# Casting the high weight parts a group ahead of the low parts in a hybrid retention and RWKV-7 decoder step

## The chip, the core and the metric

One NeuronCore of a Trainium2 chip runs the whole program in one launch. The metric is the device time in microseconds. Three runs of the kernel before gave 2919.16, 2921.64 and 2923.35 us; the median is 2921.64 us. Five engines work in parallel, each in the order of its own queue: TensorE (PE, with its weight loads as PEld), VectorE (DVE), ScalarE (ACT), GpSimd (POOL) and SyncE (SP), which issues every DMA here. An instruction whose semaphores are not there yet holds up everything behind it on its engine.

## The reference

Two layers of a decoder run on 256 new positions of one sequence and on 8 decode tokens, 264 columns in all, in float32. Cut to what matters:

```
xn = rms_norm(h, g_attn)
proj = xn @ w_mix                         # retention q, k, v, gate; RWKV r, k, v and low-rank inputs
y_ret = retention_mixer(...)              # 8 heads of 128, chunks of 128
y_rw = rwkv7_mixer(...)                   # 16 heads of 64, S = S*w + sa (kk*a)^T + v k^T
h = h + concat(y_ret, y_rw) @ w_out
hn = rms_norm(h, g_ffn)
h = h + (silu(hn @ w_gate) * (hn @ w_up)) @ w_down
```

The outputs are the normalised h and the new states of both mixers and of the token shift.

## The kernel before

**The weight stream.** All weights lie in DRAM as 128x128 blocks in the order of use, 6624 of them. `Stream` loads eight at a time (512 KB, tile `w_raw`) and splits them four at a time; four blocks are called a group here. ACT casts a group to the high part `w_hi` in float32r (L96), then DVE takes `w_raw` minus `w_hi` as the low part `w_lo` (L99; POOL for the first four groups). TensorE multiplies each block in three passes: high part by the high part of the activations (L285 or L306), high part by their low part (L286 or L307), low part by their high part (L287 or L308). `proj` (16 blocks per output tile) and `contract` do this.

**The rings.** `w_raw`, `w_hi` and `w_lo` have three buffers each. At the first block of group c, `next` calls `make` for group c+2: its cast and its subtraction stand there in the queues of ACT and DVE, one after the other. With three buffers, the cast for c+2 writes where group c-1 lay, so it waits until TensorE has done the second pass of the last block of c-1; the subtraction waits for the cast.

**The mixers.** Everything else is a generator that yields the number of blocks to let pass before it issues its next instructions; `tick` runs them after every block. So the blocks set the order on all engines, and the mixer's instructions stand in the same in-order queues as the casts and subtractions. `g_seq` is the sequential part of RWKV: eight head pairs of two layers, four chunks of 64 positions each, 64 rounds. A round makes the right-hand side `rT` from PSUM tile `py` in two quarters, one by DVE (L574) and one by ACT (L575), both into one tile; one block later ACT copies `oc` (L577); TensorE multiplies `rT` (L587), ACT copies `Z1` (L590), TensorE multiplies (L594), DVE subtracts into `r1` (L597), TensorE multiplies (L601), and so on, with `yield 3` or `yield 1` between the steps. `g_pair` prepares a pair (L419, L426 to L456, L435), `g_norm` normalises (L706 to L718), `adder` adds a PSUM tile to h (L1244).

**The stages of one layer.** Projections with both mixers, then w_out, then the FFN in four quarters, in the first of which the decode state is updated on POOL (`g_update`).

Of the kernel before, what the change touches and what calls it, by code (L numbers as in the profile page):

```python
# [11 lines left out]
F32 = mybir.dt.float32  # L12
# [25 lines left out]
R_DECAY, R_AAA, R_GATE, R_MV = 64, 64, 160, 32  # L38
PAST = 2048
RC = 8  # L40
RAW_BUFS = 3
CH = 4
HL_BUFS = 3
CAP = {"st": 3, "pw": 5, "qa": 2, "qb": 2, "qc": 2, "gy": 2, "blk": 27, "TM": 8, "y": 1}
TA, RR, LV, UB, U2 = 4, 2, 2, 6, 4
NORM_EPS = 1e-6
# [26 lines left out]


class Stream:
    def __init__(self, nc, pools, src, ahead):
        self.nc, self.pools, self.src = nc, pools, src
        self.n = src.shape[0] * RC // CH
        self.raw, self.ready = {}, {}
        self.loaded = self.made = self.pos = 0  # L80
        self.ahead = ahead

    def load(self):
# [2 lines left out]
        self.raw[self.loaded] = w  # L86
        self.loaded += 1

    def make(self):
        nc = self.nc  # L90
        r, i = divmod(self.made, RC // CH)
        while self.loaded < min(self.src.shape[0], r + RAW_BUFS):
            self.load()
        w = self.raw[r][:, i * CH:(i + 1) * CH]
        h = self.pools[1].tile([P, CH, P], F32R, name="w_hi")
        nc.scalar.activation(out=h, in_=w, func=AF.Copy)  # L96
        l = self.pools[2].tile([P, CH, P], F32R, name="w_lo")
        eng = nc.gpsimd if self.made < KB // CH else nc.vector
        eng.tensor_tensor(out=l, in0=w, in1=h.bitcast(F32), op=ALU.subtract)  # L99
        self.ready[self.made] = (h, l)  # L100
        self.made += 1

    def next(self):
        c, i = divmod(self.pos, CH)
        while self.made < min(self.n, c + 1 + self.ahead):
            self.make()
        self.ready.pop(c - 1, None)
        h, l = self.ready[c]
        self.pos += 1
        return h[:, i], l[:, i]  # L110


class Task:
# [2 lines left out]


class Kern:
    """The main flow emits the weight stream: each 128x128 block is split into two float32r parts and multiplies the
    split activations in three passes. Every mixer step is a generator that yields the number of stream blocks to let  # L120
    pass before its next instructions, so that they reach the in-order engines when their operands are there."""

    def __init__(self, ctx, tc, a, o):
        self.tc, self.nc, self.a, self.o, self.ctx = tc, tc.nc, a, o, ctx
        nc = self.nc

        def pool(name, bufs=1, **kw):
            return ctx.enter_context(tc.tile_pool(name=name, bufs=bufs, **kw))

        self.const = pool("const")  # L130
        self.blk = pool("blk", bufs=CAP["blk"])
        self.st = pool("st", bufs=CAP["st"], space=PSUM)
        self.pw = pool("pw", bufs=CAP["pw"], space=PSUM)
        self.rp = pool("rp", bufs=2)
        self.sm = pool("sm", bufs=4)
        self.un = pool("un", bufs=3)
        self.de = pool("de", bufs=4)
        self.dr = pool("dr", bufs=2, space=DRAM)
        self.stream = Stream(nc, (pool("w_raw", RAW_BUFS), pool("w_hi", HL_BUFS), pool("w_lo", HL_BUFS)), a["ws"],
                             HL_BUFS - 1)  # L140
# [417 lines left out]
    def g_seq(self, l, p, sv, AR, cf, LA, KA, TM, bv, Y):  # L558
        nc, rp, un = self.nc, self.rp, self.un
        XT = sv["XT"]  # L560
        m1 = self.masked(LA, 1, "m1", 1)
        o = rp.tile([P, 2, P], F32, name="o", tag="o", bufs=2)
        S = None
        lo, hi = slice(0, 64), slice(64, 128)
        for c in range(NC):
            ar = AR[:, c].rearrange("p a b -> p (a b)")
            bT, kT, vT = (TM[i][:, c] for i in range(3))
            py = yield from self.pget()
            nc.tensor.matmul(py[:, 0:P], lhsT=KA[:, c], rhs=vT, start=True, stop=c == 0)
            if c > 0:  # L570
                nc.tensor.matmul(py[:, 0:P], lhsT=ar, rhs=S, start=False, stop=True)
            yield 1
            rT = self.rT[:, c % 2]
            nc.vector.tensor_scalar(out=rT[lo, lo], in0=py[lo, lo], scalar1=-1.0, scalar2=None, op0=ALU.mult)  # L574
            nc.scalar.activation(out=rT[hi, hi], in_=py[lo, hi], func=AF.Copy, scale=-1.0)  # L575
            oc = un.tile([P, P], F32, name="oc", tag="u", bufs=UB)
            nc.scalar.activation(out=oc[hi], in_=py[hi, 0:P], func=AF.Copy)  # L577
            self.pput()
            ct = cf[:, c, CW:CW + 1]
            if c > 0:  # L580
                sc = un.tile([P, P], F32, name="Sc", tag="u", bufs=UB)
                nc.scalar.activation(out=sc, in_=S, func=AF.Copy, scale=ct)
            pS = yield from self.pget()
            nc.tensor.matmul(pS[:, 0:P], lhsT=kT, rhs=vT, start=True, stop=False)
            yield 3
            pz = yield from self.pget()
            nc.tensor.matmul(pz[:, 0:P], lhsT=XT[:, c], rhs=rT, start=True, stop=True)  # L587
            yield 1
            Z1 = un.tile([P, P], F32, name="Z1", tag="u", bufs=UB)
            nc.scalar.activation(out=Z1, in_=pz[:, 0:P], func=AF.Copy)  # L590
            self.pput()
            yield 3
            pl = yield from self.pget()
# [12 lines left out]
            yield 3
            nc.tensor.matmul(pS[:, 0:P], lhsT=bT, rhs=Z, start=False, stop=True)
            yield 1
            Sn = un.tile([P, P], F32, name="S", tag="S", bufs=2)
            if c == 0:  # L610
                nc.scalar.activation(out=Sn, in_=pS[:, 0:P], func=AF.Copy, scale=ct)
            else:
                nc.vector.scalar_tensor_tensor(out=Sn, in0=pS[:, 0:P], scalar=ct, in1=sc, op0=ALU.mult, op1=ALU.add)
            self.pput()
            S = Sn
            po = yield from self.pget()
            nc.tensor.matmul(po[:, 0:P], lhsT=LA[:, c], rhs=Z, start=True, stop=True)
            yield 1
            nc.vector.tensor_tensor(out=o[64 * (c % 2):64 * (c % 2) + 64, c // 2], in0=po[hi, 0:P], in1=oc[hi],
                                    op=ALU.add)  # L620
            self.pput()
            yield 2
        for hh in range(2):
            s = slice(64 * hh, 64 * hh + 64)
            nc.sync.dma_start(out=self.o["srp"][l, 2 * p + hh], in_=S[s, s])
        self.rel("TM", "TM", "TM")
        self.spawn(self.g_out(l, p, o, bv, Y), 1, "out")
# [503 lines left out]
    def layer(self, l):  # L1131
        nc = self.nc
        if l == 0:
            self.xt = []
            self.load_prev(0)
            self.stream.ahead = 0
            for k in range(KB):
                if k % 2 == 0:
                    self.new_h(k // 2)
                    nc.sync.dma_start(out=self.hp[k // 2], in_=self.a["x"][k // 2])  # L1140
                    if k % 4 == 0 and k < 4 * RAW_BUFS:
                        self.stream.load()
                self.xt.append(self.spawn(self.g_split(k, "g_attn", None, None, True), 1 + k))
            self.consts()
            self.sumsq = [self.spawn(self.g_sumsq(k, None, True, (lambda: self.rel("TM")) if k % 2 == 1 else None),
                                     KB // 2 + k, "sumsq") for k in range(KB)]
# [10 lines left out]
        lora = []  # L1157
        for j in range(3):
            lora.append(self.spawn(self.g_lora(l, j, self.proj(TP)), 1, "mix"))
            self.stream.ahead = HL_BUFS - 1  # L1160
        self.Y = [{} for _ in range(16)]
        yt = [[] for _ in range(16)]
        pds, rds, free = [], [], None
# [258 lines left out]

# [11 lines left out]
```

## Time and profile before

| | |
|---|---|
| runs, median | 2921.64 us (2919.16 to 2923.35) |
| span of the profiled execution | 2925.0 us |
| PE busy | 2799.1 us (96%) |
| DVE busy | 2009.9 us (69%) |
| ACT busy | 1416.1 us (48%) |
| POOL busy | 806.9 us (28%) |
| DMA | 512.50 MB, mean 175 GB/s |

The profiled execution has no time beside its span; the span is 3.4 us above the median of the runs and 1.6 us above the slowest of them. Matmuls overlap: a row gives one as 0.28 us, yet in the FFN they start 0.12 us apart, so busy time is a union and what is left of the span is idle time. Rows of waits say which engine and line ended an engine's idle time.

### The profile page before, as it was taken

Reading aid. Unit: us, or ns where it says so; the run is one execution under the profiler, and the core shown is the slowest. Engines: PE = TensorE matmul, PEld = TensorE weight load, DVE = VectorE, ACT = ScalarE, POOL = GpSimd, SP = SyncE. Lnnn points to the kernel's source line nnn. Section 1 sums busy time; section 2 is a strip of 40 time slices with the busy share of each in tenths; the row PEclk is TensorE's granted clock in tenths of the full one; section 3 lists DMA queues with packets and bytes.
Section 4 is the critical chain, followed back from the end, with each engine's and each line's share of the span. In section 5 each row is a group of like instructions: output and inputs, shape, how many; then the busy total and the mean of one; then the engine's idle time right before and its main releaser. Section 6 shows DMA issues by size and latency. Waiting matters only on the chain. (4 is left out here: it accounts for less than half of the span.)

```text
span 2925.0 us, 59208 instructions
## 1 busy us (share of the span) xinstructions
PE 2799.1 (96%) x22298; PEld 2755.2 (94%) x22298; DVE 2009.9 (69%) x3964; ACT 1416.1 (48%) x2823; POOL 806.9 (28%) x1316
## 2 busy tenths in 40 slices
PE   7998999999999999999999999999999999999998
PEld 7998999899999999999998888888999999999998
DVE  6677777887856656556766777778877565565665
ACT  5544455445444444444545445544544444444444
POOL 4545555434400000000234556554243000000002
PEclk9999999999999999999999999999999999999999
DMA  4454555565655555555654445556656555555554
GB/s 161 142 155 148 157 153 173 189 221 191 203 182 179 180 179 180 180 180 181 211 158 137 150 146 156 160 163 212 203 193 195 181 180 181 180 181 179 181 180 148
DMA packets 230832, 512.50 MB, mean 175 GB/s; under 512 B 57488, under 2 KB 105872, under 8 KB 230544
## 3 DMA queue, kind: packets, MB, share of 16 engines
q1 hardware_dynamic: 230544, 508.70, 54.6%
q8 instruction: 175, 2.87, 0.4%
q14 instruction: 113, 0.93, 0.1%
HBM read 485.24 MB, written 23.38 MB: 174 GB/s over the span
## 5 line engine op out<-in xcount | busy, mean ns | idle before, releaser
L99 DVE TENSOR_TENSOR w_lo<-w_raw,w_hi 128x512 fp32r<-128x512 f32 x1652 | 1240.4, 753 | 849.3 <-ACT w_hi L96 835.8
L96 ACT ACTIVATE w_hi<-w_raw 128x512 fp32r<-128x512 f32 x1656 | 1042.8, 631 | 1131.5 <-PE st L286 631.1
L285 PE MATMUL st<-blk,w_hi 128*128 128x264 f32 (+1 forms) x4704 | 1438.6, 306 | 11.9 <-ACT w_hi L96 7.4
L287 PE MATMUL st<-blk,w_lo 128*128 128x264 f32 (+1 forms) x4704 | 1353.0, 288 | 15.5 <-DVE w_lo L99 14.7
L286 PE MATMUL st<-blk,w_hi 128*128 128x264 f32 (+1 forms) x4704 | 1351.4, 287 | 1.0 <-DVE blk L1094 1.0
L287 PEld LDWEIGHTS st<-blk,w_lo 128*128 128x128 f32 x4704 | 895.0, 190 | 22.8 <-DVE w_lo L99 21.3
L285 PEld LDWEIGHTS st<-blk,w_hi 128*128 128x128 f32 x4704 | 896.2, 191 | 17.1 <-ACT w_hi L96 11.0
L286 PEld LDWEIGHTS st<-blk,w_hi 128*128 128x128 f32 x4704 | 898.0, 191 | 3.9 <-DVE blk L1094 2.0
L306 PE MATMUL st<-blk,w_hi 128*128 128x264 f32 x1920 | 551.0, 287 | 5.8 <-DVE h L1244 4.5
L307 PE MATMUL st<-blk,w_hi 128*128 128x264 f32 x1920 | 548.6, 286 | 0.0
L308 PE MATMUL st<-blk,w_lo 128*128 128x264 f32 x1920 | 546.7, 285 | 0.0
L1035 POOL TENSOR_TENSOR acc<-acc,sq 128x264 f32<-128x264 f32 x73 | 62.7, 860 | 1374.7 <-ACT sq L1032 1374.3
L306 PEld LDWEIGHTS st<-blk,w_hi 128*128 128x128 f32 x1920 | 361.0, 188 | 8.8 <-issue 4.0
L308 PEld LDWEIGHTS st<-blk,w_lo 128*128 128x128 f32 x1920 | 362.5, 189 | 0.1
L307 PEld LDWEIGHTS st<-blk,w_hi 128*128 128x128 f32 x1920 | 361.4, 188 | 0.1
L684 POOL TENSOR_TENSOR sv_t<-sv_m,sv_x 32x15 f32<-32x15 f32 (+7 forms) x240 | 90.0, 375 | 27.1 <-DMA sv_m<-scr_l 13.7
L1244 DVE TENSOR_TENSOR h<-h,st 128x264 f32<-128x264 f32 x224 | 94.1, 420 | 2.9 <-PE st L308 2.8
L686 POOL TENSOR_TENSOR sv_x<-sv_x,sv_t 32x15 f32<-32x15 f32 (+7 forms) x240 | 85.2, 355 | 18.8
L575 ACT ACTIVATE c_rT<-pw 64x64 f32<-64x64 f32 x64 | 13.8, 215 | 113.3 <-DVE c_rT L574 113.1
L323 ACT ACTIVATE mix_d<-mix_p,c_vec 128x256 f32<-128x256 f32 x54 | 27.5, 508 | 71.8 <-DVE mix_p L319 44.6
L899 POOL TENSOR_TENSOR qkb<-rS,qkb 128x512 f32<-128x512 f32 x32 | 44.5, 1391 | 58.9 <-DVE rS L896 58.9
L816 POOL TENSOR_TENSOR uS<-uS,dec_v 128x512 f32<-128x512 f32 x16 | 23.7, 1480 | 113.0 <-DMA uS<-in_s_rwkv 113.0
(251 smaller groups left out, 2636.5 us busy)
## 6 DMA issues: line engine op xcount, KB each, us to landing
w_raw<-in_ws SPq DMA_DIRECT2D x828, 512.0 KB
qkb<-scr_qk SPq DMA_DIRECT2D x64, 256.0 KB
rS<-in_s_ret SPq DMA_DIRECT2D x32, 256.0 KB
out_sts<-rS SPq DMA_DIRECT2D x32, 256.0 KB
h<-in_x SPq DMA_DIRECT2D x16, 264.0 KB
dS<-in_s_rwkv SPq DMA_DIRECT2D x16, 256.0 KB
uS<-in_s_rwkv SPq DMA_DIRECT2D x16, 256.0 KB
out_srs<-uS SPq DMA_DIRECT2D x16, 256.0 KB
```

The lines of the kernel that those rows point to most:

```text
L96: nc.scalar.activation(out=h, in_=w, func=AF.Copy)
L99: eng.tensor_tensor(out=l, in0=w, in1=h.bitcast(F32), op=ALU.subtract)
L285: nc.tensor.matmul(ps, lhsT=hi, rhs=self.x[k][:, 0, 0:n], start=k == 0, stop=False)
L286: nc.tensor.matmul(ps, lhsT=hi, rhs=self.x[k][:, 1, 0:n], start=False, stop=False)
L287: nc.tensor.matmul(ps, lhsT=lo, rhs=self.x[k][:, 0, 0:n], start=False, stop=k == KB - 1)
L306: nc.tensor.matmul(ps, lhsT=hi, rhs=t[:, 0, 0:T], start=k == 0, stop=False)
L307: nc.tensor.matmul(ps, lhsT=hi, rhs=t[:, 1, 0:T], start=False, stop=False)
L308: nc.tensor.matmul(ps, lhsT=lo, rhs=t[:, 0, 0:T], start=False, stop=k == n - 1)
L684: nc.gpsimd.tensor_tensor(out=t, in0=bc(M[:, j, j + 1:SB], 2, j + 1), in1=bc(X0[:, j, 0:j + 1], 1, m), op=ALU.mult)
L686: nc.gpsimd.tensor_tensor(out=X0[:, j + 1:SB, 0:j + 1], in0=X0[:, j + 1:SB, 0:j + 1], in1=t, op=ALU.subtract)
L1035: nc.gpsimd.tensor_tensor(out=self.acc, in0=self.acc, in1=sq, op=ALU.add)
L1244: self.nc.vector.tensor_tensor(out=h, in0=h, in1=ps, op=ALU.add)
```

## The change

The stream keeps the high and the low parts in two dictionaries and makes them apart. At the first block of group c the cast for group c+3 is issued; the subtraction for group c+2 is issued at the third block of group c. `w_hi` has five buffers, `w_lo` four and `w_raw` four. With ahead 0, which holds for the first projection alone, cast and subtraction of group c stand at its first block as before. A `w_raw` load is still issued where the tile two before it begins to be cast, which stands one group earlier than before. The first quarter of `rT` is made by ACT too. The program's `dynamic_dma_scratch_size` is set to 1024. Lines after the class move down by 7 or 8: L96 is L102, L99 is L109, L574 is L581.

```diff
-RAW_BUFS = 3
+RAW_BUFS = 4
-HL_BUFS = 3
+HI_BUFS, LO_BUFS = 5, 4
+AHEAD = 2
...
-    def make(self):
-        r, i = divmod(self.made, RC // CH)
-        while self.loaded < min(self.src.shape[0], r + RAW_BUFS):
-            self.load()
-        w = self.raw[r][:, i * CH:(i + 1) * CH]
-        h = self.pools[1].tile([P, CH, P], F32R, name="w_hi")
-        nc.scalar.activation(out=h, in_=w, func=AF.Copy)
-        l = self.pools[2].tile([P, CH, P], F32R, name="w_lo")
-        eng = nc.gpsimd if self.made < KB // CH else nc.vector
-        eng.tensor_tensor(out=l, in0=w, in1=h.bitcast(F32), op=ALU.subtract)
+    def make_hi(self, c):
+        while self.his <= min(c, self.n - 1):
+            r = self.his // (RC // CH)
+            while self.loaded < min(self.src.shape[0], r + RAW_BUFS - 1):
+                self.load()
+            h = self.hi[self.his] = self.pools[1].tile([P, CH, P], F32R, name="w_hi")
+            self.nc.scalar.activation(out=h, in_=self.part(self.his), func=AF.Copy)
+            self.his += 1
+    def make_lo(self, c):
+        while self.los <= min(c, self.n - 1):
+            l = self.lo[self.los] = self.pools[2].tile([P, CH, P], F32R, name="w_lo")
+            eng = self.nc.gpsimd if self.los < KB // CH else self.nc.vector
+            eng.tensor_tensor(out=l, in0=self.part(self.los), in1=self.hi[self.los].bitcast(F32), op=ALU.subtract)
+            self.los += 1
     def next(self):
         c, i = divmod(self.pos, CH)
-        while self.made < min(self.n, c + 1 + self.ahead):
-            self.make()
+        self.make_hi(c + self.ahead + (self.ahead > 0))
+        self.make_lo(c + self.ahead - (i < CH // 2 and self.ahead > 0))
...
-            nc.vector.tensor_scalar(out=rT[lo, lo], in0=py[lo, lo], scalar1=-1.0, scalar2=None, op0=ALU.mult)
+            nc.scalar.activation(out=rT[lo, lo], in_=py[lo, lo], func=AF.Copy, scale=-1.0)
             nc.scalar.activation(out=rT[hi, hi], in_=py[lo, hi], func=AF.Copy, scale=-1.0)
...
-    nc = bacc.Bacc("TRN2", target_bir_lowering=False, num_devices=1)
+    nc = bacc.Bacc("TRN2", target_bir_lowering=False, num_devices=1,
+                   dynamic_dma_scratch_size=1024)
```

The orders of TensorE and POOL are the same instruction for instruction; those of DVE, ACT and SP move. On DVE, at the start of the fourth head pair of the first layer (`o` ends a round of `g_seq`, `rv` to `q` and `AR` are retention's v and the pair's preparation, `bst` to `bve` a norm), before:

```order
L99 TENSOR_TENSOR w_lo<-w_raw,w_hi 128x512
L619 TENSOR_TENSOR o<-pw,oc 64x128
L850 TENSOR_TENSOR rv<-st,c_R 128x264
L853 TENSOR_TENSOR v_3905<-st,c_R 128x8
L426 SCALAR_TENSOR_TENSOR q_3929<-ta,mix_k 128x264
L429 SCALAR_TENSOR_TENSOR AR<-mix_k,c_vec,cf 128x4x64
L574 TENSOR_SCALAR c_rT<-pw 64x64
L706 BN_STATS bst<-o 128x6 x4
L99 TENSOR_TENSOR w_lo<-w_raw,w_hi 128x512
L709 BN_AGGR bmv<-bst 128x2 x4
```

And the same piece of DVE's queue in the changed kernel:

```order
L109 TENSOR_TENSOR w_lo<-w_raw,w_hi 128x512
L620 SCALAR_TENSOR_TENSOR S<-pw,cf,Sc 128x128
L626 TENSOR_TENSOR o<-pw,oc 64x128
L857 TENSOR_TENSOR rv<-st,c_R 128x264
L860 TENSOR_TENSOR v_3905<-st,c_R 128x8
L109 TENSOR_TENSOR w_lo<-w_raw,w_hi 128x512
L433 SCALAR_TENSOR_TENSOR q_3931<-ta,mix_k 128x264
L436 SCALAR_TENSOR_TENSOR AR<-mix_k,c_vec,cf 128x4x64
L713 BN_STATS bst<-o 128x6 x4
L716 BN_AGGR bmv<-bst 128x2 x4
```

Each subtraction stands two blocks later, and the quarter of `rT` (L574) is gone from DVE. A little further down the same queue, up to the `r1` of that round (`dn`, `di`, `AR`, `rk` belong to the pair's preparation), before:

```order
L439 SCALAR_TENSOR_TENSOR bdb<-q_3929,c_hv,ic 64x4x64 x2
L99 TENSOR_TENSOR w_lo<-w_raw,w_hi 128x512
L446 TENSOR_SCALAR dn<-pw 64x2 x4
L450 RECIPROCAL di<-dn 128x4
L454 TENSOR_TENSOR AR<-mix_r,cf 128x4x64
L456 SCALAR_TENSOR_TENSOR rk<-mix_r,c_vec,km 128x264
L597 TENSOR_TENSOR r_4011<-c_rT,pw 128x128
L99 TENSOR_TENSOR w_lo<-w_raw,w_hi 128x512 x2
```

And in the changed kernel:

```order
L109 TENSOR_TENSOR w_lo<-w_raw,w_hi 128x512
L446 SCALAR_TENSOR_TENSOR bdb<-q_3931,c_hv,ic 64x4x64 x2
L453 TENSOR_SCALAR dn<-pw 64x2 x4
L457 RECIPROCAL di<-dn 128x4
L461 TENSOR_TENSOR AR<-mix_r,cf 128x4x64
L463 SCALAR_TENSOR_TENSOR rk<-mix_r,c_vec,km 128x264
L109 TENSOR_TENSOR w_lo<-w_raw,w_hi 128x512
L604 TENSOR_TENSOR r_4013<-c_rT,pw 128x128
L109 TENSOR_TENSOR w_lo<-w_raw,w_hi 128x512
```

Between `rv` and `r1` three subtractions stand now where two stood. On ACT, at the same round (`cf`, `ic`, `sqk` are the pair's), before:

```order
L411 ACTIVATE cf<-cum 128x260
L413 ACTIVATE ic<-cum 128x256
L424 ACTIVATE sqk<-mix_k,c_vec 128x256
L575 ACTIVATE c_rT<-pw 64x64
L577 ACTIVATE oc<-pw 64x128
L96 ACTIVATE w_hi<-w_raw 128x512
L590 ACTIVATE Z_3979<-pw 128x128
```

And in the changed kernel:

```order
L418 ACTIVATE cf<-cum 128x260
L420 ACTIVATE ic<-cum 128x256
L431 ACTIVATE sqk<-mix_k,c_vec 128x256
L581 ACTIVATE c_rT<-pw 64x64
L582 ACTIVATE c_rT<-pw 64x64
L584 ACTIVATE oc<-pw 64x128
L102 ACTIVATE w_hi<-w_raw 128x512
L597 ACTIVATE Z_3983<-pw 128x128
```

The two quarters of `rT` follow each other on ACT, and the cast behind them is that of the group after.

## Rows read from the trace of the kernel before

**Rows 1.** The page's first part: busy time, share, instructions of each engine.
```profile
PE 2799.1 (96%) x22298; PEld 2755.2 (94%) x22298; DVE 2009.9 (69%) x3964; ACT 1416.1 (48%) x2823; POOL 806.9 (28%) x1316
```

**Rows 2.** Windows by stage: length, busy (instructions) by engine, granted clock, DMA share, GB/s.
```profile
75.00:600.00 525.00, 483.72 (x3782) 469.14 (x3781) 394.27 (x905) 255.61 (x609) 278.48 (x515) 0.98 0.53 162
600.00:825.00 225.00, 220.38 (x1773) 217.13 (x1772) 177.04 (x281) 111.74 (x205) 83.48 (x80) 1.00 0.62 199
825.00:1425.00 600.00, 600.00 (x4911) 600.00 (x4911) 361.14 (x639) 283.37 (x486) 4.55 (x6) 1.00 0.56 181
...
1500.00:2040.00 540.00, 497.48 (x3856) 480.33 (x3856) 407.27 (x935) 263.36 (x619) 286.76 (x521) 0.98 0.51 159
2040.00:2250.00 210.00, 203.32 (x1622) 199.92 (x1621) 168.83 (x266) 103.83 (x194) 86.12 (x86) 0.99 0.62 197
```

**Rows 3.** PE's waits, whole span: who waited for whom, us in total, times, longest.
```profile
PE pw L601 <- DVE r L597: 22.1, 20, 2.4
PE pw L587 <- ACT c_rT L575: 19.0, 17, 3.0
PE st L287 <- DVE w_lo L99: 14.7, 22, 1.8
PE pw L419 <- DVE AR L454: 10.2, 10, 1.9
...
PE pw L571 <- DVE S L613: 5.0, 5, 3.0
```

**Rows 4.** Waits of DVE and ACT, whole span.
```profile
DVE w_lo L99 <- ACT w_hi L96: 835.8, 1276, 4.0
ACT w_hi L96 <- PE st L286: 631.1, 705, 4.3
...
ACT c_rT L575 <- DVE c_rT L574: 113.1, 60, 5.2
```

**Rows 5.** DVE's waits from 75 to 600 us.
```profile
DVE w_lo L99 <- ACT w_hi L96: 108.6, 117, 3.7
```

**Rows 6.** PE's waits from 600 to 825 us.
```profile
PE st L287 <- DVE w_lo L99: 4.1, 6, 1.2
```

**Rows 7.** PE's waits from 2040 to 2250 us.
```profile
PE st L287 <- DVE w_lo L99: 6.0, 6, 1.8
```

**Rows 8.** Groups by line: count, busy us, mean ns, idle before and releasers.
```profile
L99 DVE TENSOR_TENSOR w_lo<-w_raw,w_hi 128x512 fp32r<-128x512 f32 x1652 | 1240.4, 753 | 849.3 <-ACT w_hi L96 835.8 <-PE pw L356 2.2 <-PE st L287 1.7
...
L574 DVE TENSOR_SCALAR c_rT<-pw 64x64 f32<-64x64 f32 x64 | 13.6, 212 | 3.1 <-PE pw L571 2.0
```

**Rows 9.** DVE in order of time, 282.5 to 293 us: start, length, instruction, idle before.
```profile
287.55 0.69 DVE L99 TENSOR_TENSOR w_lo<-w_raw,w_hi 128x512 fp32r<-128x512 f32 x1 [0.72 <-ACT w_hi L96]
...
291.88 0.29 DVE L597 TENSOR_TENSOR r<-c_rT,pw 128x128 f32<-128x128 f32 x1
```

**Rows 10.** ACT in order of time, same stretch.
```profile
286.35 0.22 ACT L575 ACTIVATE c_rT<-pw 64x64 f32<-64x64 f32 x1 [2.03 <-DVE c_rT L574]
...
286.89 0.63 ACT L96 ACTIVATE w_hi<-w_raw 128x512 fp32r<-128x512 f32 x1
```

**Rows 11.** PE in order of time, same stretch.
```profile
286.62 0.49 PE L587 MATMUL pw<-c_rT,XT 128*128 128x128 f32 x2 [1.01 <-ACT c_rT L575]
...
292.22 0.49 PE L601 MATMUL pw<-r,XT 128*128 128x128 f32 x2 [1.50 <-DVE r L597]
```

**Rows 12.** Windows of 3.4 us, columns as in rows 2.
```profile
100.40:103.80 3.40, 3.40 (x17) 3.40 (x16) 3.35 (x3) 0.00 (x0) 3.08 (x4) 0.50 0.51 155
...
414.40:417.80 3.40, 3.40 (x31) 3.40 (x30) 2.38 (x7) 0.89 (x2) 0.76 (x1) 1.00 0.09 12
...
2148.40:2151.80 3.40, 3.24 (x14) 3.01 (x14) 2.92 (x6) 1.59 (x5) 0.00 (x0) 0.50 0.47 147
```

**Rows 13.** DVE's subtractions alone in two stretches, columns DVE, POOL, clock, DMA.
```profile
75.00:600.00 525.00, 177.84 (x222) 0.00 (x0) 0.98 0.53 162
...
825.00:1425.00 600.00, 283.34 (x410) 0.00 (x0) 1.00 0.56 181
```

More of the change, by code (lines that the diff above doesn't have):

```diff
@@ L78, in __init__ @@
         self.n = src.shape[0] * RC // CH
-        self.raw, self.ready = {}, {}
-        self.loaded = self.made = self.pos = 0
+        self.raw, self.hi, self.lo = {}, {}, {}
+        self.loaded = self.his = self.los = self.pos = 0
         self.ahead = ahead
@@ L87, in load, with part @@
         self.loaded += 1
-    def make(self):
-        nc = self.nc
-        r, i = divmod(self.made, RC // CH)
-        while self.loaded < min(self.src.shape[0], r + RAW_BUFS):
-            self.load()
-        w = self.raw[r][:, i * CH:(i + 1) * CH]
-        h = self.pools[1].tile([P, CH, P], F32R, name="w_hi")
-        nc.scalar.activation(out=h, in_=w, func=AF.Copy)
-        l = self.pools[2].tile([P, CH, P], F32R, name="w_lo")
-        eng = nc.gpsimd if self.made < KB // CH else nc.vector
-        eng.tensor_tensor(out=l, in0=w, in1=h.bitcast(F32), op=ALU.subtract)
-        self.ready[self.made] = (h, l)
-        self.made += 1
+    def part(self, c):
+        r, i = divmod(c, RC // CH)
+        return self.raw[r][:, i * CH:(i + 1) * CH]
+    def make_hi(self, c):
[12 more added lines that the diff above has]
+            self.los += 1
     def next(self):
         c, i = divmod(self.pos, CH)
-        while self.made < min(self.n, c + 1 + self.ahead):
-            self.make()
-        self.ready.pop(c - 1, None)
-        h, l = self.ready[c]
+        self.make_hi(c + self.ahead + (self.ahead > 0))
+        self.make_lo(c + self.ahead - (i < CH // 2 and self.ahead > 0))
         self.pos += 1
-        return h[:, i], l[:, i]
+        return self.hi[c][:, i], self.lo[c][:, i]
 class Task:
@@ L138, in __init__ @@
         self.dr = pool("dr", bufs=2, space=DRAM)
-        self.stream = Stream(nc, (pool("w_raw", RAW_BUFS), pool("w_hi", HL_BUFS), pool("w_lo", HL_BUFS)), a["ws"],
-                             HL_BUFS - 1)
+        self.stream = Stream(nc, (pool("w_raw", RAW_BUFS), pool("w_hi", HI_BUFS), pool("w_lo", LO_BUFS)), a["ws"],
+                             AHEAD)
         self.tasks, self.pos, self.used, self.last = [], 0, dict.fromkeys(CAP, 0), {}
@@ L1140, in layer @@
                     nc.sync.dma_start(out=self.hp[k // 2], in_=self.a["x"][k // 2])
-                    if k % 4 == 0 and k < 4 * RAW_BUFS:
+                    if k % 4 == 0 and k < 12:
                         self.stream.load()
@@ L1159, in layer @@
             lora.append(self.spawn(self.g_lora(l, j, self.proj(TP)), 1, "mix"))
-            self.stream.ahead = HL_BUFS - 1
+            self.stream.ahead = AHEAD
         self.Y = [{} for _ in range(16)]
```

## The prediction

> **What bounds the kernel now.** I read the page's first part, then windows by stage, then PE's waits, then those of DVE and ACT, and last one stretch in order of time. PE is busy 2799.1 of 2925.0 us [rows 1], so 125.9 us of idle time are all that a change of waits can win at an unchanged clock. The windows [rows 2] say where it lies. In the FFN (825 to 1425 us) PE is busy 600.00 of 600 us at the full clock: nothing can be won there, and the other layer's FFN reads the same. In the two mixer stretches PE is idle 525.00-483.72 = 41.3 and 540.00-497.48 = 42.5 us; in the stretches after them, which hold w_out's end and the start of the FFN with the state update, 4.6 and 6.7 us. Together 95.1 us. The remaining 30.8 us are the first loads, the last norm and the layers' border, which the change leaves alone.
>
> PE's waits [rows 3] name the culprits: L601 for DVE's r1 22.1 us in 20 waits, L587 for ACT's rT 19.0 us in 17, L287 for the low weight part 14.7, L419 10.2, L571 5.0. These five are 71.0 us of the 95.1; the smaller groups hold about 24.1. Nearly all of them end on DVE. Yet DVE is busy only 394 of 525 us in the mixer [rows 2]: it is late in bursts, not short of time. What holds it is in [rows 4]: it stands 835.8 us at the subtraction, in 1276 waits, for a cast that ACT could not start, since ACT itself stands 631.1 us for PE's second pass. With three buffers the cast for group c+2 can't begin before PE has finished group c-1, which is just where PE stands when that cast is due. So at each group DVE and ACT are tied to PE and begin whatever stands behind with a lag. In the first mixer stretch that is 108.6 us in 117 waits, 0.93 us each [rows 5].
>
> One place shows the knot. ACT stands 2.03 us at L575 for DVE's quarter of rT, which is behind a burst of DVE work [rows 10]. PE waits 1.01 us for it at L587 [rows 11]. The cast that stands behind L575 therefore starts only at 286.89 [rows 10], DVE idles 0.72 us for it although 4.3 us of its work lie between that subtraction and r1, and r1 comes at 291.88 [rows 9], for which PE waits 1.50 us at L601 [rows 11].
>
> **The change, part by part.** *rT on ACT.* It removes 64 instructions of 212 ns from DVE (13.6 us) [rows 8] and adds 64 to ACT, where such a quarter reads 0.22 us (14.1 us) [rows 10]. ACT is busy 256 of 525 us in the mixer and idles 113.1 us in all for the DVE quarter [rows 4], so the added time lies in idle time that goes; if it were not hidden it would cost 14.1 us. After it ACT waits for PE alone, and what is behind ACT's rT (oc, the cast) comes up to 5.2 us earlier. PE's 19.0 us at L587 lose their main cause. At the place shown, ACT's last work ahead of L575 ended 2.03 us before it started and two quarters are 0.4 us, so rT would be there by about 284.8, before PE asked for it at 285.61 [rows 10, 11]. Bounds 0 and 19.0; I take 14, as a cast may now stand ahead of it.
>
> *Casts a group further ahead, five and four buffers.* No instruction is added: 1652 subtractions remain on DVE [rows 8]. The cast for group c+3 needs PE to be done with c-2, the subtraction for c+2 likewise, so neither waits at its place in the queue as long as the engine isn't more than a group ahead of PE. The gate goes; what is late next is DVE's own work in a burst. For the waits on DVE's products in the mixer (L601, L419, L571: 37.3 us) the bounds are 0 and 37.3. If every wait (1.1 us on average at L601, 22.1/20) had one gate of 0.93 us ahead of it, 85% would go. At the place shown it is 0.72 of 1.50 us, 48%, and there PE would also arrive 1.01 us earlier, as L587 no longer holds it. The measured place is the nearest row: I take 45%, 17 us. Of the smaller groups, whose causes are mixed, 30%: 7 us (bounds 0 and 24.1).
>
> For the waits at L287 (14.7 us) DVE may now run one and a half groups ahead of PE's place; before, the cast began when PE was at the group. Two blocks of PE time are lost, since the subtraction is issued at the third block instead of the first: six blocks of three matmuls at 0.122 us (600 us / 4911) are 2.2 us of lead, before it was 2.9, of which the wait and the cast took more than a microsecond. Bounds 0 and 14.7; I take 11, since 10.1 of them lie in the stretches after the mixers [rows 6, 7], where DVE has few products of PE to wait for.
>
> *The clock.* Behind long waits the granted clock reads 0.50, the 1.2 GHz level, for 3.4 us: 17 and 14 matmuls start there, against 31 in such a window at 1.00 [rows 12]. Between 75 and 2250 us there are eleven such stretches, the first and the last of which stand in the rows. Each loses about 3.4 x (31-17)/31 = 1.5 us, 17 us together; the rounded means (0.98, 0.98, 0.99) [rows 2] give 23, within their rounding. They follow waits of 1.5 us and more. Bounds 0 and 17; half of those waits should fall shorter: 8 us.
>
> *Loads and the scratch.* A w_raw load is issued a group earlier into a tile freed earlier; the DMA share is 0.53 to 0.62 [rows 2], so nothing is expected either way. No DMA is issued from POOL, so I take the smaller scratch at nothing. Bound: if every transfer of the two mixer stretches slowed in step, the share of 0.53 leaves room for almost twice its time.
>
> Sum: 14 + 17 + 7 + 11 + 8 = 57 us. Against the profiled execution: 2925.0 - 57 = 2868. The median of the runs lies 3.4 us below that span, so 2921.64 - 57, some 2865 us.
>
> **Rivals.** *A: the wait moves on.* Bursts are DVE's own work: from the subtraction to the end of r1 at the place shown DVE needs 4.6 us [rows 9], while PE takes 292.22-1.50-286.62 = 4.1 us from L587 to where it asks for r1 [rows 11], and one more subtraction of 0.69 us now stands between. If PE is let through at L587, it comes to L601 earlier and waits there longer. Then L587 gives back its 14, the bursts yield a third of the 17, and the clock 3: 6 + 3 + 11 = 20 us, 2902 us. For it: subtractions take 177.84/222 = 0.80 us in the mixer against 283.34/410 = 0.69 in the FFN [rows 13], 24 us that no buffer removes, as POOL is busy 278 us there [rows 2]. Against it: the 0.93 us of idle time per gate [rows 5] are more than the 0.5 us that this burst lacks.
>
> A rule beside this: the Trainium skill, SBUF — State Buffer, Who interferes with whom, says that a DVE instruction with two SBUF inputs contends with a GpSimd instruction that reads SBUF, since the second input goes through a shared read interface. The longer subtractions while POOL works [rows 13] agree. By that rule alone no DVE time is won, and rival A would be the whole story; by the idle rows the gates go besides.
>
> *B: nearly all of it goes.* DVE without gates has a fifth of its mixer time free, runs ahead, and the bursts find it early. Then 75 of the 95.1 us and 15 of the clock go: 90 us, 2832 us. For it: the idle at the gates (108.6 us in one stretch [rows 5]) is over twice PE's 41.3. Against it: r1, S and o each wait for PE itself, so DVE cannot run far ahead in the mixer.
>
> *C: the later subtraction holds PE.* The lead of 2.2 us in the queue is less than DVE's lag in a burst (at L601 up to 2.4 us of PE's wait beyond the three blocks that it is given, 1.1 us). If PE then waits at L287 by the lost 0.73 us in each of the 117 gates of a mixer stretch, that is 85 us for one and some 170 for both; it decides from about a third of the gates on, where it eats the 57. At half of the gates: 85 - 57 = 28 us slower, 2950 us. Against it: outside the stretches of [rows 6, 7] PE waits only 14.7-10.1 = 4.6 us at L287 today, with the gate ahead of every subtraction.
>
> *D: nothing moves.* The subtraction is no longer late, but the instruction behind it waits for PE at the same moment: within 6 us of 2922.
>
> **Numbers.** Forecast 0.55, A 0.21, B 0.13, D 0.06, C 0.05. The forecast's own range, from the bounds and the shares taken, is 2840 to 2885. For 8 in 10 I leave out C, D and the lower half of B: 2830 to 2905. Two runs of this kernel differ by up to 0.14%, so 0.2% (5.8 us) is about what can be told from no change: faster 0.88, same 0.07, slower 0.05.
>
> **What would show it.** In the changed kernel DVE's wait at w_lo for w_hi should fall from 835.8 us to under 200; ACT's wait at rT should be for PE and small; L587 should all but leave PE's waits (under 5 us); L601 should be 8 to 14 us, L287 under 5; the FFN stretches should keep 0.122 us per matmul; five or six stretches at clock 0.50 should remain in the mixers. L601 at 22 us or more with L587 gone is A; L287 above 30 us is C. The forecast is wrong if PE's idle time in the two mixer stretches together stays above 65 us (then A) or falls under 25 (then B).

## The result, and the profile after

Four runs of each kernel gave a median of 2882.35 us after (2877.92 to 2884.35) against 2922.32 us before (2919.16 to 2923.35). The ratio is 0.9861, with a 95% interval of 0.9848 to 0.9874: the change saves 40.0 us, where the forecast had 57. The profiled execution spans 2879.3 us, 45.7 us less than before; the terms below are set against that number.

The page's first part shows busy time, share of the span and count, now 2777.8 us for PE against 2799.1 [rows 1]:

```profile
PE 2777.8 (96%) x22298; PEld 2746.0 (95%) x22298; DVE 1971.1 (68%) x3900; ACT 1421.9 (49%) x2887; POOL 825.5 (29%) x1316
```

So PE idles 101.5 us where it idled 125.9 (24.4 less), and it is busy 21.3 us less for the same 22298 matmuls. The windows by stage (stretch, its length, busy time and count of PE, PEld, DVE, ACT and POOL, granted clock, DMA share, GB/s) show where:

```profile
0.00:75.00 75.00, 61.42 (x403) 57.36 (x404) 54.82 (x132) 40.88 (x86) 37.07 (x63) 1.00 0.54 177
75.00:600.00 525.00, 490.19 (x3871) 479.61 (x3870) 393.53 (x893) 258.80 (x651) 290.51 (x526) 0.98 0.54 168
600.00:825.00 225.00, 218.77 (x1777) 217.32 (x1777) 174.91 (x269) 112.68 (x203) 75.92 (x65) 1.00 0.60 197
825.00:1425.00 600.00, 600.00 (x4912) 600.00 (x4910) 353.32 (x643) 290.99 (x496) 6.63 (x12) 1.00 0.57 182
...
1500.00:2040.00 540.00, 510.47 (x4029) 497.21 (x4028) 415.94 (x940) 271.12 (x671) 303.04 (x539) 0.99 0.55 171
2040.00:2250.00 210.00, 208.52 (x1699) 207.42 (x1699) 162.13 (x244) 107.80 (x196) 72.83 (x60) 1.00 0.61 197
```

Against [rows 2] the two mixer stretches idle 34.8 and 29.5 us instead of 41.3 and 42.5, the two behind them 6.2 and 1.5 instead of 4.6 and 6.7: 72.0 instead of 95.1. The later windows of the faster kernel hold somewhat later work. Counted between the same matmuls as before, which the equal order of TensorE allows, the four idle 34.8, 27.7, 6.2 and 3.3 us, the same sum. The FFN is what it was, 0.122 us per matmul. One matmul of the first mixer stretch takes 490.19/3871 = 126.6 ns on average, before it took 127.9.

PE's waits (tile waited at, engine and line waited for, us in total, times, longest) answer to [rows 3]; L285 to L287 are now L292 to L294, L587 is L594, L601 is L608, L571 is L578, L419 is L426:

```profile
PE st L294 <- DVE w_lo L109: 34.6, 31, 2.7
PE pw L608 <- DVE r L604: 19.4, 11, 4.6
...
PE st L315 <- DVE w_lo L109: 5.0, 4, 1.5
...
PE pw L578 <- DVE S L620: 2.8, 1, 2.8
PE pw L594 <- ACT c_rT L582: 2.6, 1, 2.6
...
PE pw L426 <- DVE AR L461: 1.2, 2, 0.9
```

And the waits of DVE and ACT, in the same columns, answer to [rows 4]:

```profile
ACT c_rT L581 <- PE pw L578: 78.5, 41, 3.7
...
DVE w_lo L109 <- ACT w_hi L102: 3.1, 4, 1.6
```

The gate is gone, 3.1 us instead of 835.8, and rT has all but left PE's list. In their place PE waits 34.6 us for the low weight part itself, which had been 14.7. One such place, first on DVE (start, duration, line, operation):

```profile
204.96 1.82 DVE L446 SCALAR_TENSOR_TENSOR bdb<-q,c_hv,ic 64x256 f32<-64x256 f32 x2
206.79 0.67 DVE L453 TENSOR_SCALAR dn<-pw 64x2 f32<-64x2 f32 x4
...
207.59 0.40 DVE L461 TENSOR_TENSOR AR<-mix_r,cf 128x256 f32<-128x256 f32 x1
...
208.33 2.35 DVE L109 TENSOR_TENSOR w_lo<-w_raw,w_hi 128x512 fp32r<-128x512 f32 x2
```

then on PE, with the wait ahead of an instruction in brackets:

```profile
207.20 0.28 PE L293 MATMUL st<-blk,w_hi 128*128 128x272 f32 x1
...
210.13 0.59 PE L294 MATMUL st<-blk,w_lo 128*128 128x272 f32 x1 [2.64 <-DVE w_lo L109]
```

and the window from 209.90 us on, with the columns of the windows by stage:

```profile
209.90:213.30 3.40, 3.17 (x14) 3.01 (x15) 3.30 (x9) 0.58 (x3) 0.00 (x0) 0.50 0.43 153
```

DVE hardly stops in this burst. The subtraction that PE waits for is the first of the two in the last DVE row. It stands behind 3.4 us of the burst (204.96 to 208.33). PE ends the last matmul that it can make at about 207.5 and goes on at 210.13, 1.8 us after the subtraction began. From 209.9 us on the clock reads 0.50, the 1.2 GHz level, and only 14 matmuls start in 3.4 us.

Not all of this wait is the queue. The three subtractions of this stretch (shortest, median and longest in ns), and what POOL does meanwhile, read:

```profile
L109 DVE TENSOR_TENSOR w_lo<-w_raw,w_hi x3: 679/681/1744, 208.3 to 211.9; 128x512 fp32r<-128x512 f32 x3
```

```profile
208.18 1.34 POOL L533 TENSOR_TENSOR Lm<-LA,c_m_lv 128x512 f32<-128x512 f32 x1
```

The first subtraction took 1.74 us instead of 0.68, so some 1.1 us of the 2.64 are its own length; the last section comes back to this. Of the 31 waits, 7 ended with a subtraction longer than 0.9 us, and the excess over 0.685 us accounts for at most 5.1 of the 34.6 us.

### The profile page after: what moved, and what is told of

Read it like the earlier page. It is cut to its first block, busy times and chain, and to the rows that moved or that the text cites. A ratio compares the mean times of both kernels' runs of the same rounds, so it can differ in the third digit from the quotient of the medians.

```text
span 2879.3 us, 58894 instructions
## 1 busy us (share of the span) xinstructions
PE 2777.8 (96%) x22298; PEld 2746.0 (95%) x22298; DVE 1971.1 (68%) x3900; ACT 1421.9 (49%) x2887; POOL 825.5 (29%) x1316
## 4 chain that ended last, share of the span: by engine, by line
PE 79%; DVE 10%; POOL 4%; issue 2%; DMA 2%; ACT 1%; SPq 0%; DVEq 0%; POOLq 0%; ACTq 0%
PE st L294 17%; PE st L292 17%; PE st L293 17%; PE st L314 7%; PE st L315 7%; PE st L313 7%; DVE w_lo L109 3%; POOL sv_x L693 1%; POOL sv_t L691 1%; PE pw L426 1%; PE pw L363 1%; PE pw L367 1%; PE pw L546 1%; DMA qkb<-scr_qk 1%; PE pw L608 1%
## 5 line engine op out<-in xcount | busy, mean ns | idle before, releaser
L102 ACT ACTIVATE w_hi<-w_raw 128x512 fp32r<-128x512 f32 x1656 | 1035.6, 630 | 909.6 <-PE st L293 548.2
L292 PE MATMUL st<-blk,w_hi 128*128 128x264 f32 (+1 forms) x4704 | 1435.5, 305 | 11.5 <-ACT w_hi L102 7.8
L294 PE MATMUL st<-blk,w_lo 128*128 128x264 f32 (+1 forms) x4704 | 1350.0, 287 | 35.3 <-DVE w_lo L109 34.6
L293 PE MATMUL st<-blk,w_hi 128*128 128x264 f32 (+1 forms) x4704 | 1348.3, 287 | 1.4 <-DVE blk L1101 1.3
L109 DVE TENSOR_TENSOR w_lo<-w_raw,w_hi 128x512 fp32r<-128x512 f32 x1652 | 1207.6, 749 | 161.1 <-PE st L294 115.7
L294 PEld LDWEIGHTS st<-blk,w_lo 128*128 128x128 f32 x4704 | 892.2, 190 | 42.9 <-DVE w_lo L109 41.9
L292 PEld LDWEIGHTS st<-blk,w_hi 128*128 128x128 f32 x4704 | 893.5, 190 | 16.4 <-ACT w_hi L102 10.5
L293 PEld LDWEIGHTS st<-blk,w_hi 128*128 128x128 f32 x4704 | 895.1, 190 | 4.5 <-DVE blk L1101 2.6
L315 PE MATMUL st<-blk,w_lo 128*128 128x264 f32 x1920 | 548.8, 286 | 5.4 <-DVE w_lo L109 5.0
L313 PE MATMUL st<-blk,w_hi 128*128 128x264 f32 x1920 | 550.5, 287 | 1.7 <-DVE h L1251 1.5
L315 PEld LDWEIGHTS st<-blk,w_lo 128*128 128x128 f32 x1920 | 362.5, 189 | 8.9 <-DVE w_lo L109 8.6
L313 PEld LDWEIGHTS st<-blk,w_hi 128*128 128x128 f32 x1920 | 361.1, 188 | 3.3 <-ACT w_hi L102 1.7
L1113 DVE TENSOR_TENSOR fg<-st,c_R 128x264 f32<-128x264 f32 x88 | 38.0, 432 | 171.5 <-PE st L294 168.4
L1125 DVE TENSOR_TENSOR fg<-st,fg 128x264 f32<-128x264 f32 x88 | 37.9, 431 | 52.6 <-PE st L294 52.6
L611 ACT ACTIVATE Z<-pw 128x128 f32<-128x128 f32 x64 | 17.7, 276 | 106.2 <-PE pw L608 106.1
```

What stands on the lines that cost most here:

```text
L102: self.nc.scalar.activation(out=h, in_=self.part(self.his), func=AF.Copy)
L109: eng.tensor_tensor(out=l, in0=self.part(self.los), in1=self.hi[self.los].bitcast(F32), op=ALU.subtract)
L292: nc.tensor.matmul(ps, lhsT=hi, rhs=self.x[k][:, 0, 0:n], start=k == 0, stop=False)
L293: nc.tensor.matmul(ps, lhsT=hi, rhs=self.x[k][:, 1, 0:n], start=False, stop=False)
L294: nc.tensor.matmul(ps, lhsT=lo, rhs=self.x[k][:, 0, 0:n], start=False, stop=k == KB - 1)
L313: nc.tensor.matmul(ps, lhsT=hi, rhs=t[:, 0, 0:T], start=k == 0, stop=False)
```

## The experiments

Theory 1 was that the later place of the subtraction (third block instead of first) takes back what the deeper rings give, because its lead of 2.2 us is shorter than a DVE burst. Its rivals were that the bursts are DVE's own work and late at any place, that the buffers alone do it, and that rT does. Theory 3, which came up with e5, was that the loss is a step which belongs to the place within the group. Each kernel ran four or five times. There were three sittings on three chips (e1 to e4; e5 to e8; e9 to e11), in which the kernel before stood at 2922.1, 2924.7 and 2923.4 us; between sittings the ratios to it are the safer comparison.

**e1: rT alone.** The kernel before, with both quarters on ACT:

```diff
-nc.vector.tensor_scalar(out=rT[lo, lo], in0=py[lo, lo], scalar1=-1.0, scalar2=None, op0=ALU.mult)
+nc.scalar.activation(out=rT[lo, lo], in_=py[lo, lo], func=AF.Copy, scale=-1.0)
```

> The kernel before with one edit: both quarters of rT on ACT. Stream, rings and order as before. Prediction's step: PE's 19.0 us at L587 shrink to under 5, 14 us are won, some 2908 us. Rival (the wait moves on): L587 goes too, but DVE's burst is still as long and PE meets it at L601, whose 22.1 us grow by about as much: 2916 to 2924 us. The cast that stood behind ACT's wait comes earlier under both, so DVE's wait at w_lo for w_hi falls by some 30 us at most from 835.8.

Measured: 2911.79 us, ratio 0.9967 (0.9954 to 0.9980), 10 us. PE's waits:

```profile
PE pw L601 <- DVE r L597: 31.9, 19, 3.4
...
PE st L287 <- DVE w_lo L99: 14.6, 24, 1.8
...
PE pw L587 <- ACT c_rT L575: 3.7, 5, 1.9
```

Of the 19.0 us for rT [rows 3] 3.7 are left, but 9.8 us come back at the next DVE product, L601 (22.1 to 31.9 us). The time lies between what the prediction's step and the rival had expected. The gate all but keeps its size:

```profile
DVE w_lo L99 <- ACT w_hi L96: 818.4, 1272, 4.0
```

**e2: the stream alone.** The changed kernel with the first quarter back on DVE, the reverse of e1's edit.

> The changed kernel with the first quarter of rT put back on DVE. If the parts add up as the prediction had them, 14 us are lost against the changed kernel: 2896 us, with L587's counterpart (L594) back at some 15 us or more of PE's waits. If the wait only moves on, the time is within 5 us of the changed kernel's 2882, with L594 up and L608 and L294 down by as much. DVE's wait at w_lo for w_hi stays near 10 us either way.

Measured: 2885.25 us, 0.9872 (0.9859 to 0.9886): 3 us from the whole change, with intervals that overlap.

```profile
PE st L294 <- DVE w_lo L109: 26.2, 22, 2.6
PE pw L594 <- ACT c_rT L582: 16.1, 13, 3.8
...
PE pw L608 <- DVE r L604: 13.7, 15, 1.7
```

With the stream as changed, PE waits 16.1 us for rT and 13.7 for r1; with rT on ACT it is 2.6 and 19.4, and 34.6 instead of 26.2 at L294. These three add up to 56.0 us here and 56.6 with rT on ACT: what rT no longer holds, the two waits behind it do.

**e3: the subtraction at the first block.** The changed kernel with one line different:

```diff
-self.make_lo(c + self.ahead - (i < CH // 2 and self.ahead > 0))
+self.make_lo(c + self.ahead)
```

> The changed kernel with the subtraction for group c+2 issued at the first block of group c instead of the third; rings, casts and rT as changed. Theory 1 (the late subtraction costs): PE's waits at w_lo (34.6 at L294 and 5.0 at L315) fall to about the 14.7 of before, the other waits stay, 2882 - 25 = 2857 to 2865 us. Theory 2 (bursts are DVE's own work, and the place of the subtraction only decides at which instruction PE meets it): waits at w_lo fall, those at r1 (L608, 19.4 us), AR and S rise by as much, 2876 to 2886 us.

Measured: 2855.55 us, 0.9773 (0.9759 to 0.9786), 27 us below the changed kernel. PE's waits and the mixers' windows:

```profile
PE pw L608 <- DVE r L604: 21.9, 14, 4.1
PE pw L426 <- DVE AR L461: 9.0, 7, 1.9
...
PE st L294 <- DVE w_lo L109: 7.6, 12, 1.3
...
PE pw L578 <- DVE S L620: 2.3, 1, 2.3
```

```profile
75.00:600.00 525.00, 497.19 (x3960) 488.03 (x3959) 402.57 (x912) 263.04 (x657) 288.78 (x527) 0.98 0.56 173
...
1500.00:2040.00 540.00, 514.50 (x4077) 502.95 (x4076) 418.48 (x951) 275.07 (x676) 292.13 (x506) 0.99 0.56 174
```

L294 falls from 34.6 to 7.6 us, the mixers' idle time from 64.3 to 27.8 + 25.5 = 53.3. The later issue of the subtraction is what takes back; the time is a little under theory 1's range. Theory 2 is out by the time, but not wholly by the waits: L608 and L426 together rise from 20.6 to 30.9 us.

**e4: the buffers, without the cast's step.** The changed kernel's rings and rT, but cast and subtraction both two groups ahead, at the first block, as before:

```diff
-self.make_hi(c + self.ahead + (self.ahead > 0))
-self.make_lo(c + self.ahead - (i < CH // 2 and self.ahead > 0))
+self.make_hi(c + self.ahead)
+self.make_lo(c + self.ahead)
```

> The changed kernel's rings (5 high, 4 low, 4 raw) and rT on ACT, but cast and subtraction of group c+2 together at the first block of group c, as in the kernel before. If the buffers alone take the gate away, the time is that of e3 within 4 us and DVE's wait at w_lo for w_hi stays under 50 us. If the cast has to stand a group ahead, because ACT comes late to it behind its own waits for PE, DVE waits for w_hi by 50 to 250 us in all and the time is 10 to 20 us above e3.

Measured: 2880.63 us, 0.9855 (0.9842 to 0.9869), as fast as the whole change. DVE's wait for the cast, then PE's waits:

```profile
DVE w_lo L109 <- ACT w_hi L102: 207.4, 245, 4.7
```

```profile
PE pw L608 <- DVE r L604: 27.1, 19, 3.4
PE pw L426 <- DVE AR L461: 10.5, 10, 1.9
PE st L294 <- DVE w_lo L109: 9.3, 15, 2.1
```

Beside e1, which has the same rT, more buffers (with the scratch, which e4 has too) take the gate from 818.4 to 207.4 us, and 31.2 us from the time. The cast a group ahead then gives 25.1 more (e4 to e3), where 10 to 20 were expected, and the subtraction two blocks later takes 26.8 back (e3 to the changed kernel).

**e5: the subtraction at the fourth block.**

```diff
-self.make_lo(c + self.ahead - (i < CH // 2 and self.ahead > 0))
+self.make_lo(c + self.ahead - (i < CH - 1 and self.ahead > 0))
```

> The changed kernel with the subtraction for group c+2 at the fourth block of group c, one block (0.37 us) later than in the change and three later than in e3. Theory 1 (its lead in the queue is what PE waits for): e3 to the change was two blocks for 27 us, so one more costs about as much again per block: 2890 to 2900 us, waits at w_lo 50 to 60 us. Theory 3 (the loss belongs to the first block alone, where cast and subtraction stand together): 2878 to 2885 us.

Measured: 2884.31 us, 0.9877 (0.9860 to 0.9893).

```profile
PE st L294 <- DVE w_lo L109: 37.3, 29, 3.6
```

Against the changed kernel, one block less of lead costs 2 us by the medians and 5 by the ratios, whose intervals overlap. This is theory 3's range; the loss is not in proportion to the lead.

**e6: the third block, four blocks more lead.** One more low buffer, and the subtraction for the group after next but one:

```diff
-HI_BUFS, LO_BUFS = 5, 4
+HI_BUFS, LO_BUFS = 5, 5
-self.make_lo(c + self.ahead - (i < CH // 2 and self.ahead > 0))
+self.make_lo(c + self.ahead + (i >= CH // 2 and self.ahead > 0))
```

> The changed kernel with the subtraction for group c+3 at the third block of group c and five low buffers: two blocks more of lead than e3, casts as changed. Theory 1 carried on: waits at w_lo fall from e3's 7.6 us to under 3 and the time is some 5 us under e3, 2848 to 2853 us; but the cast for c+3 stands only two blocks ahead of it, so DVE's wait for w_hi may come back as in e4. If it does (over 50 us), 2856 to 2866 us.

Measured: 2872.96 us, 0.9826 (0.9811 to 0.9841), a miss: slower than both ranges. DVE's wait, then PE's:

```profile
DVE w_lo L109 <- ACT w_hi L102: 354.7, 548, 3.2
```

```profile
PE pw L608 <- DVE r L604: 26.4, 14, 6.1
...
PE st L294 <- DVE w_lo L109: 2.8, 4, 1.2
```

The wait at L294 goes (2.8 us left), but the cast is now issued only two blocks ahead of its subtraction, so the gate is back, and L608 stands at 26.4 us (21.9 in e3). The run changed two things at once and could not part place from lead; e10 does.

**e7: everything a group deeper, at the first block.**

```diff
-HI_BUFS, LO_BUFS = 5, 4
+HI_BUFS, LO_BUFS = 6, 5
-self.make_hi(c + self.ahead + (self.ahead > 0))
-self.make_lo(c + self.ahead - (i < CH // 2 and self.ahead > 0))
+self.make_hi(c + self.ahead + 2 * (self.ahead > 0))
+self.make_lo(c + self.ahead + (self.ahead > 0))
```

> Everything one group further than e3: cast for c+4 and subtraction for c+3 at the first block of group c, six high and five low buffers. If the lead of casts and subtractions is what is left, waits at w_lo vanish and 2842 to 2850 us follow. If what is left is DVE's own bursts behind PE's products (L608 21.9 us, L426 9.0 us in e3), no more than the 7.6 us at w_lo can go and those two stay within a third: 2848 to 2858 us.

Measured: 2850.69 us, 0.9753 (0.9739 to 0.9766), the fastest kernel of the study: 72 us below the one before, 32 below the changed one.

```profile
PE pw L608 <- DVE r L604: 23.3, 14, 4.0
PE pw L426 <- DVE AR L461: 14.0, 7, 3.5
```

No wait at L294 for DVE's subtraction stands in the list any more. What is left are above all the waits for r1 (L608, 21.9 us in e3) and AR (L426, 9.0 in e3), which the added depth did not shorten. The time is in the second range, though AR's wait grew by more than a third; over e3 it is 5 us, and the two intervals still overlap.

**e8: more room for r1.** e3, and two blocks more between r1's subtraction and its product:

```diff
-yield 3
+yield 5
```

> The kernel of e3 with five blocks instead of three between r1's subtraction and the product that reads it (L608), nothing else. If PE's wait there is DVE's lag beyond the slack given (three blocks are 1.1 us, the waits are 0.1 to 4.1 us), two more blocks take up to 0.73 us from each of the 14 waits: L608 falls from 21.9 to 10 to 14 us and the time to 2843 to 2850 us. If the wait moves on to the next product of DVE (S at L578, AR at L426), the sum of PE's waits stays and so does the time, 2851 to 2860 us. A longer round (64 rounds of two more blocks) costs nothing unless the last pair comes late to w_out, which would show as waits at L313 above the 4.1 us of e3.

Measured: 2864.2 us, 0.9794 (0.9778 to 0.9811): a miss, with no gain over e3. It is 9 us slower by the medians and 6 by the ratios, whose intervals overlap.

```profile
PE st L313 <- DVE h L1251: 12.4, 9, 2.8
PE pw L608 <- DVE r L604: 9.7, 7, 4.1
...
PE st L313 <- POOL blk L835: 7.2, 2, 4.7
```

L608 does fall, from 21.9 to 9.7 us, but each round of the recurrence is two blocks longer, the mixer's outputs come later, and PE waits for them at the next matrix (L313, 12.4 and 7.2 us). So the waits cancel: PE idles 84.4 us in all, in e3 83.0. The rest of what parts the two profiled executions is PE's busy time, 2779.9 us against 2769.8, which these waits do not explain. Part of it lies in the second layer's FFN, which the edit doesn't touch, e3 first:

```profile
2400.00:2600.00 200.00, 200.00 (x1642) 200.00 (x1641) 119.73 (x210) 94.90 (x159) 0.00 (x0) 1.00 0.55 181
```

```profile
2400.00:2600.00 200.00, 200.00 (x1631) 200.00 (x1631) 118.27 (x208) 94.14 (x159) 0.00 (x0) 1.00 0.55 179
```

**e9: the second block.**

```diff
-self.make_lo(c + self.ahead - (i < CH // 2 and self.ahead > 0))
+self.make_lo(c + self.ahead - (i < 1 and self.ahead > 0))
```

> The changed kernel with the subtraction for group c+2 at the second block of group c, between e3 (first, 2855.6 us) and the change (third, 2882.4 us). Theory 1 (its lead is what counts, block by block): half of the 27 us, 2865 to 2872 us, waits at w_lo about 20 us. Theory 3 (a step, since only at the first block does it stand ahead of the mixer's instructions of that group): 2877 to 2885 us, waits at w_lo above 30 us.

Measured: 2877.82 us, 0.9843 (0.9829 to 0.9857).

```profile
PE st L294 <- DVE w_lo L109: 17.5, 16, 2.1
```

From first to fourth block: 2855.6, 2877.8, 2882.4, 2884.3 us, by ratio 0.9773, 0.9843, 0.9861, 0.9877. PE's wait at L294 grows with each block (7.6, 17.5, 34.6, 37.3), as theory 1 had it, but of the time 22 of 29 us are lost at the first step, as theory 3 had it. Only that step is clear of the intervals.

**e10: e7 with its subtraction at the third block.**

```diff
-self.make_lo(c + self.ahead + (self.ahead > 0))
+self.make_lo(c + self.ahead + (i >= CH // 2 and self.ahead > 0))
```

> The kernel of e7 (cast for c+4, six and five buffers) with the subtraction for group c+3 at the third block of group c: the place of the change, with four blocks more lead, and the cast six blocks ahead, so that the gate of e6 is gone. Theory 1: the lead is two blocks more than e3's, so waits at w_lo stay under 5 us and the time is at or under e3's, 2848 to 2856 us. Theory 3 (the place within the group decides): it stays as far from e7 as the change from e3, 2868 to 2880 us.

Measured: 2859.47 us, 0.9780 (0.9767 to 0.9793).

```profile
PE pw L608 <- DVE r L604: 22.9, 13, 4.3
...
PE st L294 <- DVE w_lo L109: 0.3, 1, 0.3
```

The time lies between the two ranges, nearer to theory 1's. The wait at L294 is all but gone. With the changed kernel's place in the queue but four blocks more lead, and casts early enough, 23 of the 27 us are back: most of the loss was lead. Against e7, at the first block and with two blocks more of lead, 9 us stay, which the wait at L294 (0.3 us) cannot hold.

**e11: e3 with the first rT quarter on DVE**, by e1's edit reversed.

> The kernel of e3 with the first quarter of rT back on DVE. rT on ACT was worth 10 us in e1 and 3 us on top of the change (e2). If it is worth what DVE's bursts still hold, the gates being gone: 2857 to 2861 us. If the 3 us of e2 came from the late subtractions, which held PE anyway: 2864 us or more, with PE's waits at L594 back at over 10 us.

Measured: 2857.25 us, 0.9773 (0.9759 to 0.9787), e3's ratio to the last digit.

```profile
PE pw L608 <- DVE r L604: 13.8, 12, 2.1
PE pw L594 <- ACT c_rT L582: 12.9, 11, 2.5
```

The 21.9 us at L608 and 1.2 at L594 of e3 stand here as 13.8 + 12.9: the wait has only moved. The time is in the first range and L594 above the second one's 10 us. Beside an early subtraction, rT on ACT is worth nothing that these runs can measure.

## Why the prediction was right in direction and short in size

PE's idle time in the four stretches fell by 95.1 - 72.0 = 23.1 us where 14 + 17 + 7 + 11 = 49 were forecast. By the terms of the sum, with the waits of the whole span as in the prediction and "all the rest" as what they leave of the stretches' idle time:

| term | waits before | after | won | forecast |
|---|---|---|---|---|
| rT (L587, now L594) | 19.0 | 2.6 | 16.4 | 14 |
| DVE's products (L601, L419, L571, now L608, L426, L578) | 37.3 | 23.4 | 13.9 | 17 |
| low part (L287, now L294) | 14.7 | 34.6 | -19.9 | 11 |
| all the rest | 24.1 | 11.4 | 12.7 | 7 |
| sum | 95.1 | 72.0 | 23.1 | 49 |

*The gate.* As forecast: w_lo's wait for w_hi was to be under 200 us and is 3.1. e4 shows that buffers and rT together are worth 41 us, of which e1 has 10 for rT.

*DVE's products.* Right in size (13.9 of 17), but by luck. L608 alone, at 19.4, is above the 8 to 14 forecast, and the other two take up the difference. In e3, which differs only in the earlier subtraction, the three hold 21.9 + 9.0 + 2.3 = 33.2 us, 4.1 less than before, and in e7 39.6, without any gate or wait at L294 to speak of. So the lag at these products did not go with the gate, as the 45% had it. About ten of the 13.9 us were won only while PE stood at L294.

*L287, "I take 11": the step that failed.* The wait for the low part was to fall by 11 us and rose by 19.9, a miss of 30.9 us, more than the whole shortfall; in the smaller groups L315 adds 5.0 of the same kind. The working had the number that decides, a lead cut from 2.9 to 2.2 us, but set against it only the cast's delay, which went, and not a burst on DVE. In the burst shown, 3.4 us stand ahead of the subtraction, which then takes 1.1 us longer than most. The reason given, that 10.1 of the waits at L287 lie behind the mixers, was drawn from a kernel in which the gate held DVE level with PE. Behind the mixers they did fall, to 6.2 us; inside them they rose from 3.1 to 26.0. L287 above 30 us was the sign set for C, and this is rival C's mechanism, at 31 places instead of half of all gates: too few to make the kernel slower, enough to cost 27 us against the same kernel with the subtraction at the first block (e3). By e10, four blocks more lead give most of it back.

*rT, "I take 14".* The wait was won, the time was not: 10 us alone (e1), 3 on top of the stream (e2), none beside an early subtraction (e11). PE passes L594 earlier and stands at L608 or L294 instead. ACT's wait at rT is for PE, as forecast, but 78.5 us and not small. Rival A said this of rT, and there it was right. The 14 were taken out of a wait without asking how soon DVE's next product follows.

*The clock (8 us).* Five or six half-clock stretches were to remain of eleven; nine lengths of 3.4 us do, two of them in one piece. Of these eight stretches three begin beside a wait at L294, four beside one at L608 and one beside one at L594. That count gives 3 us. The rest came from the first 75 us, which the forecast left out. Before, they held a half-clock stretch three lengths long, worth 4.5 us at the prediction's price; the changed kernel holds none there:

```profile
38.90:49.10 10.20, 8.93 (x41) 8.64 (x40) 4.42 (x11) 2.74 (x7) 3.17 (x7) 0.50 0.40 125
```

Together 7.5 us: the 8 that was forecast, by luck, from another place.

*Busy time, which had no term.* PE is busy 21.3 us less for the same matmuls in the same order, so the two traces can be set beside each other matmul by matmul. 7.3 of the 21.3 us lie at matmuls that stand at the half clock in one of the traces, 10.8 at others that stand within two places of a wait in one of them, and 3.3 at all the rest. By this profile a wait thus costs more than its idle time: the last matmul ahead of it counts with its whole 0.28 us (L293 in the place shown), where one in a stream adds 0.12. Against the profiled execution 57 us were forecast and 45.7 came, 11.3 less. The waits fell 25.9 short, busy time brought 13.3 more than the 8 for the clock, and 1.3 us of idle time went outside the four stretches. So the total is closer than its terms, and that is luck.

*The other rivals.* B, under which nearly all of the idle time goes, did not come with this change, but e7's 2850.69 us goes 63% of the way from the measured time to B's 2832: most of the time is there, behind the issue of one instruction and one more buffer in each of its two rings. D is out. The mixers' idle time of 64.3 us lies just inside the bound of 65 set for A, so the result stands between the forecast and A, by C's mechanism. (A's own sum of 20 us leaves out the 7 for the smaller groups without a reason.)

*What stays open.* Why the place costs 9 us where lead is ample (e7 against e10), and why the step from the first block to the second costs 22 us while the wait at L294 grows by 10. The pages and clocks of the profiled executions say where the time is, but not why. From e7 to e10 PE idles 4.8 us more and is busy 6.3 us more, with eleven half-clock lengths ahead of the last norm instead of eight. From e3 to e9 it idles 14.6 us more and is busy 7.1 us more, with twelve lengths instead of nine. At the prediction's 1.5 us each, three lengths are 4.5 us of either. A subtraction that stands just ahead of the recurrence's products in DVE's queue could explain the further waits, but was not shown. How far POOL's work lengthens DVE's other instructions was not measured. The smaller scratch and the fourth raw buffer were not tried alone.

## What to carry to other kernels

When a chain of two engines off the critical path (here cast, then subtraction) is tied to the consumer's progress by its ring, more buffers and an earlier first half free both engines; keep the second half as early in its queue as before, with more lead than the bursts that can stand ahead of it. Here six blocks, 2.2 us, were too few, and ten, some 3.7 us, with casts early enough, left 0.3 us of waits (e10). In an in-order queue, a lead of blocks is to be compared with bursts, not with mean load: DVE was 75% busy and still up to 2.7 us late. And a wait that is taken from one product of a busy engine is only won if the next product of the same engine isn't due right behind it; look at the next wait before counting the first.

## What the runs showed of the hardware

One instruction of one shape varied by a factor of nearly four. The row groups the subtractions of the changed kernel (count, then shortest, median and longest duration in ns, when, and shape):

```profile
L109 DVE TENSOR_TENSOR w_lo<-w_raw,w_hi x1652: 657/685/2476, 26.0 to 2858.6; 128x512 fp32r<-128x512 f32 x184
```

The median is 685 ns and the longest 2476. The trace also shows beside what they stretch. During 1183 of the 1652 no POOL instruction ran, and these took 657 to 697 ns. During the other 469 one did, and these took 910 ns on average; all 222 that are longer than 697 ns are among them. Together that is 105 us of DVE time. The longest, at 1603.7 us, ran beside three of POOL's TENSOR_TENSORs, one behind the other, and the one that held PE in the burst shown above ran beside POOL's L533. In the kernel before it is the same: 657 to 696 ns without POOL, 920 on average with it. This is the loss that rival A named and that no buffer removes. No run moved POOL's work away, so what that would save is not known.
